# A decoder trunk step with the FFN's gate and up projections done as pairs of tiles by seven quarter products

## The chip, the cores and the metric

The kernel runs on one core of a Trainium2 chip. Its time is the device time of one execution in microseconds (us). PE is the matmul engine, DVE the vector engine (VectorE), ACT the scalar engine (ScalarE), POOL GpSimd, SP the engine whose queue issues the DMAs. L173 is line 173 of the kernel before.

## The reference, cut to what matters

Two layers of a decoder trunk are computed for 512 prompt tokens and 8 x 8 sample tokens, 576 columns in all, in float32. Layer 0 has a Conformer and window attention mixer, layer 1 a Mamba-2 mixer. Each layer ends with the same feed-forward block (FFN), with D_MODEL = 1024 and D_FF = 2816 (22 tiles of 128):

```python
def conv_ffn(h, hist, w_gate, w_up, conv_w, conv_b, w_down):
    gate = h @ w_gate
    padded = jnp.concatenate([hist, gate], axis=1)
    gc = causal_dwconv(padded, conv_w, conv_b)
    y = (jax.nn.silu(gc) * (h @ w_up)) @ w_down
    return y, padded[:, -(FFN_CONV_WIDTH - 1):]
```

h is the RMS-normalised input, and the convolution along the tokens has three taps.

## The kernel before

Channels lie on the 128 partitions and the 576 tokens along the free axis, cut into two halves of 288 (HALF). The residual stream x is 8 tiles of 128x576. Every large product is made of three matmuls: operand and weight are each split into a high part in float32r (a copy on ACT) and a low part (the difference, on DVE), and `mm3` (L167) adds high x high (L173), high x low (L174) and low x high (L175) over the input blocks.

A weight tile of 128x1024 comes by one DMA on SP's queue into one of three raw tiles (`wr`, L152). `weights` (L157) makes its high part on ACT (L163, tile `wh`) and its low part on DVE (L164, tile `wl`); `wh` and `wl` have three buffers each.

`units` (L270) computes output tiles: for each, eight input blocks, two halves, three matmuls, thus 48 matmuls of 128x288, into PSUM banks that take turns (`pm`, ring "mm" of four). In the FFN (L312) the input pairs `self.h` are x times the norm's gain, and the norm's factor per token, `rs`, is applied when a tile leaves PSUM. `gate_evac` (L322) multiplies by rs into `gbuf` (L329, L333, L334), runs the three taps on DVE (L339, then L341 twice), the SiLU on ACT (L344, L345) and multiplies by rs once more for the up branch (L347). `up_evac` (L351) multiplies the up tile into it (L354) and splits y into a pair (L193, L194). Gates run three tiles ahead of ups. After 8, 15 and 22 tiles (PARTS, L24) `out_proj` (L290) adds the part's share of the down projection to x: 16 tiles, each added on DVE at L288. In layer 0 the last part also computes the next norm.

The program is written in an order; the framework then orders each engine's instructions once, at build time, by that order and by when it takes operands to be ready, and sets the semaphores. The order on an engine can differ from the written one, unless a matmul is held by `keep_in_program_order`. Small tiles come from a list of numbered slots (`S`, `free`), where the slot that was freed first is taken first.

## Time and profile before

| | |
|---|---|
| median of 3 runs | 1552.0 us (1550.88 to 1556.76) |
| profiled execution, span | 1551.3 us; the page gives no other time of it |
| PE busy | 1520.5 us, 11635 matmuls |
| DVE busy | 1018.5 us, 1805 instructions |
| ACT busy | 649.3 us, 1232 instructions |
| first FFN | about 220 to 632 us of the span |
| second FFN | 1127 to 1548 us of the span |

Matmuls overlap in PE's pipeline, so a matmul's listed duration is longer than the distance to the next one, and PE's busy time doesn't tell whether it is at its peak; the distance between starts does. The same holds in part for DVE.

### The profile page before, as it was taken

How to read it: one execution, taken by the hardware profiler on the slowest of the kernel's cores; microseconds unless marked ns; L12 is line 12 of the kernel's file. 1: busy time of each engine (PE TensorE's matmuls, PEld its weight loads, DVE VectorE, ACT ScalarE, POOL GpSimd, SP SyncE). 2: the span in 40 equal slices, each digit the busy share in tenths (PEclk: the TensorE clock that was granted, in tenths of full speed). 3: DMA queues.
4: the chain of work that ended last, by engine and by line, in shares of the span. 5: the costliest groups of instructions: out<-in, count | busy, mean ns of one | idle time of the engine just before them, and what ended most of it. 6: DMA issues, size and time to landing. Idle time of an engine off the chain costs nothing.

```text
span 1551.3 us, 28549 instructions
## 1 busy us (share of the span) xinstructions
PE 1520.5 (98%) x11635; PEld 1449.8 (93%) x11635; DVE 1018.5 (66%) x1805; ACT 649.3 (42%) x1232; POOL 154.7 (10%) x365
## 2 busy tenths in 40 slices
PE   8999999999999999999999999999999999999999
PEld 7977799999999999898988988998999999999999
DVE  7969887553555464678896786777976644663552
ACT  6356553221222222486855654646632222321220
POOL 0036001000000000011211112102010000000000
PEclk9999999999999999999999999999999999999999
DMA  8515223222222222136245245245222222223222
GB/s 239 136 42 131 85 70 98 86 86 85 83 77 78 92 82 85 55 104 202 71 148 180 83 115 185 72 125 173 87 84 85 91 83 82 82 73 92 82 87 75
DMA packets 69938, 157.80 MB, mean 102 GB/s; under 512 B 19871, under 2 KB 24607, under 8 KB 69807
## 3 DMA queue, kind: packets, MB, share of 16 engines
q1 hardware_dynamic: 69806, 155.97, 33.2%
q8 instruction: 92, 1.51, 0.4%
q14 instruction: 40, 0.32, 0.1%
HBM read 140.73 MB, written 15.21 MB: 101 GB/s over the span
## 4 chain that ended last, share of the span: by engine, by line
PE 88%; DVE 5%; ACT 4%; DMA 2%; issue 1%; SPq 0%; ACTq 0%; DVEq 0%
PE mm L173 27%; PE mm L175 27%; PE mm L174 26%; DMA acb<-acd 2%; PE yp L1148 1%; DVE wl L164 1%; ACT acb L1116 1%; PE mm L594 1%; ACT wh L163 1%; PE pst L1081 1%; PE pt L1063 1%; ACT sm L661 1%; PE py L1133 1%; PE pst L1200 1%; DMA out_ssm_s<-h 1%
## 5 line engine op out<-in xcount | busy, mean ns | idle before, releaser
L173 PE MATMUL mm<-hh,wh 128*128 128x288 f32 x2272 | 677.8, 299 | 6.8 <-ACT wh L163 5.5
L174 PE MATMUL mm<-hl,wh 128*128 128x288 f32 x2272 | 673.9, 297 | 0.7 <-DVE hl L389 0.4
L175 PE MATMUL mm<-hh,wl 128*128 128x288 f32 x2272 | 673.3, 297 | 0.5 <-DVE wl L164 0.4
L163 ACT ACTIVATE wh<-wr 128x1024 fp32r<-128x1024 f32 (+2 forms) x215 | 223.3, 1039 | 544.6 <-PE mm L174 275.1
L173 PEld LDWEIGHTS mm<-hh,wh 128*128 128x128 f32 x2272 | 428.3, 189 | 16.0 <-ACT wh L163 6.0
L174 PEld LDWEIGHTS mm<-hl,wh 128*128 128x128 f32 x2272 | 429.0, 189 | 4.8 <-issue 1.8
L175 PEld LDWEIGHTS mm<-hh,wl 128*128 128x128 f32 x2272 | 428.7, 189 | 3.2 <-issue 1.4
L164 DVE TENSOR_TENSOR wl<-wr,wh 128x1024 fp32r<-128x1024 f32 (+2 forms) x215 | 258.6, 1204 | 73.0 <-ACT wh L163 71.4
L173 PE MATMUL mm<-yh,wh 128*128 128x288 f32 x960 | 285.9, 298 | 1.5 <-DVE x L288 1.4
L175 PE MATMUL mm<-yh,wl 128*128 128x288 f32 x960 | 284.2, 297 | 1.3 <-DVE wl L164 1.3
L174 PE MATMUL mm<-yl,wh 128*128 128x288 f32 x960 | 285.3, 297 | 0.0
L173 PEld LDWEIGHTS mm<-yh,wh 128*128 128x128 f32 x960 | 181.1, 189 | 5.7 <-DVE x L288 2.5
L175 PEld LDWEIGHTS mm<-yh,wl 128*128 128x128 f32 x960 | 181.1, 189 | 2.4 <-DVE wl L164 1.6
L174 PEld LDWEIGHTS mm<-yl,wh 128*128 128x128 f32 x960 | 181.2, 189 | 1.5 <-issue 1.0
L288 DVE TENSOR_TENSOR x<-x,mm 128x288 f32<-128x288 f32 x192 | 84.9, 449 | 143.0 <-PE mm L175 142.8
L333 DVE TENSOR_TENSOR gbuf<-mm,rs 128x224 f32<-128x224 f32 x44 | 17.2, 391 | 108.6 <-PE mm L175 108.6
L344 ACT ACTIVATE gsilu<-gconv,par 128x512 f32<-128x512 f32 x44 | 31.8, 724 | 115.1 <-DVE gconv L341 115.1
L341 DVE SCALAR_TENSOR_TENSOR gconv<-gbuf,par,gconv 128x592 f32<-128x592 f32 x88 | 73.1, 831 | 1.5
L354 DVE TENSOR_TENSOR gsilu<-mm,gsilu 128x288 f32<-128x288 f32 x88 | 40.0, 454 | 50.5 <-PE mm L175 50.5
L880 DVE SCALAR_TENSOR_TENSOR cconv<-cbuf,par,cconv 128x600 f32<-128x600 f32 x72 | 59.6, 838 | 10.1 <-ACT cconv L878 9.5
L336 POOL COPY fpo<-gbuf 128x2 f32<-128x2 f32 x44 | 12.4, 281 | 476.0 <-DVE gbuf L333 476.0
L1116 ACT ACTIVATE acb<-acb,ac 128x128 f32<-128x128 f32 x128 | 41.4, 390 | 35.6 <-DMA acb<-acd 25.0
(322 smaller groups left out, 1593.6 us busy)
## 6 DMA issues: line engine op xcount, KB each, us to landing
wr<-in_w_gate SPq DMA_DIRECT2D x44, 512.0 KB, 3.5
wr<-in_w_up SPq DMA_DIRECT2D x44, 512.0 KB, 3.5
wr<-in_w_in_o SPq DMA_DIRECT2D x40, 512.0 KB, 3.6
wr<-in_w_down SPq DMA_DIRECT2D x32, 448.0 KB, 3.3
wr<-in_w_down SPq DMA_DIRECT2D x16, 512.0 KB, 3.5
h<-in_h SPq DMA_DIRECT2D x32, 256.0 KB, 3.1
acb<-acd SPq DMA_DIRECT2D x32, 256.0 KB, 4.2
out_ssm_s<-h SPq DMA_DIRECT2D x32, 256.0 KB, 2.6
```

What stands on the lines that cost most here:

```text
L163: nc.scalar.activation(hi[:, a:b], raw[:, a:b], AF.Copy)
L164: nc.vector.tensor_tensor(lo[:, a:b], raw[:, a:b], hi[:, a:b].bitcast(F32), op=SUB)
L173: nc.tensor.matmul(out, hi[:, ws], xh[:, sl], start=i == 0, stop=False)
L174: nc.tensor.matmul(out, hi[:, ws], xl[:, sl], start=False, stop=False)
L175: nc.tensor.matmul(out, lo[:, ws], xh[:, sl], start=False, stop=i == n - 1)
L288: nc.vector.tensor_tensor(self.x[m][:, sl], self.x[m][:, sl], p[:, :HB], op=ADD)
L333: nc.vector.tensor_tensor(g[:, 290:514], p[:, 0:224], rs[:, HB:NP], op=MUL)
L341: nc.vector.scalar_tensor_tensor(cv[:, :592], g[:, k:592 + k], w(k), cv[:, :592], op0=MUL, op1=ADD)
L344: nc.scalar.activation(sl[:, :NP], cv[:, :NP], AF.Silu, bias=b)
L354: nc.vector.tensor_tensor(sl[:, HALF[half]], p[:, :HB], sl[:, HALF[half]], op=MUL)
L880: nc.vector.scalar_tensor_tensor(cv[:, :600], g[:, k:600 + k], w(k), cv[:, :600], op0=MUL, op1=ADD)
L1116: nc.scalar.activation(acb[:, cs], acb[:, cs], AF.Relu, bias=ac[:, o:o + 1], scale=-1.0)
```

## The change

Six tiles of each FFN are computed as before: gates 0 to 3 and ups 0 and 1. All other gate and up tiles are computed in pairs f, f+1. The pair's weights are seen as a 2x2 matrix of quarters A11, A12 (tile f, input blocks 0-3 and 4-7), A21, A22 (tile f+1), and the input as quarters B11, B21 (blocks 0-3 and 4-7, first half of the tokens), B12, B22 (second half). Strassen's scheme in Winograd's form needs seven products of quarters instead of eight. Each is 4 blocks x 3 matmuls of 128x288.

- `combine` makes, once per FFN, the seven quarters of the input from the normalised x (with rs): four as they are or as differences (B11, B21, B22, T1), then T2, T3, T4, each split into high and low. Its three stages stand between the lead tiles.
- Per pair, `load` makes four sums of weight quarters (S1 to S4) on DVE; seven quarters are split (the upper tile as one tile of 1024, A22 by itself, S1 and S2 in one tile, S4 and S3 in one).
- Two products accumulate on each of the banks z, y and x, where x takes three (P6, P7, P4); between them DVE or ACT reads what is there (`r`, `e`, `a`). The gate and up evacuations become sums; the first convolution tap goes from DVE to ACT; rs drops out for the tiles from 2 on.
- The products of two successive pairs are interleaved: P1 new, P3 and P7 old, P2 and P5 new, P4 old, P6 new. The down projection is in parts of 4, 4, 4, 4 and 6 tiles. The first four are cut into 16 single tiles each, and a tile is put after P1, P3, P7 and P5 once a part of y is complete; the first matmul of each product and of each such tile keeps its place in the order. The last part goes through `out_proj` as before.
- A down weight tile now holds two output tiles of four blocks and comes by two DMAs. The "mm" ring has six banks in the FFN.

```diff
-PARTS = ((0, 8), (8, 15), (15, 22))
+LEAD_G, LEAD_U = 4, 2
+PARTS = ((0, 4), (4, 8), (8, 12), (12, 16), (16, 22))
...
+class Strassen:
+    def __init__(self, b, job, n):
+        self.b, self.nc, self.job = b, b.nc, job
+        s = b.sr
+        self.r, self.e, self.a = s[0][:, HALF[n % 2]], s[1][:, HALF[0]], s[1][:, HALF[1]]
+    def load(self):
+        b, nc = self.b, self.nc
+        low, up = b.weights_load(self.job.src[1], 1024), b.weights_load(self.job.src[0], 1024)
+        a11, a12, a21, a22 = up[:, 0:512], up[:, 512:1024], low[:, 0:512], low[:, 512:1024]
+        self.up = up
+        s1, s2, s3, s4 = self.s = [b.S(f"st{i}", 512) for i in range(4)]
+        nc.vector.tensor_tensor(s1, a21, a22, op=ADD)
+        self.d = b.S("dh", 512, F32R), b.S("dl", 512, F32R)
+        self.split(a22, *self.d)
+        nc.vector.tensor_tensor(s3, a11, a21, op=SUB)
+        nc.vector.tensor_tensor(s2, s1, a11, op=SUB)
+        nc.vector.tensor_tensor(s4, a12, s2, op=SUB)
+    def split(self, src, hi, lo):
+        nc = self.nc
+        nc.scalar.activation(hi, src, AF.Copy)
+        nc.vector.tensor_tensor(lo, src, hi.bitcast(F32), op=SUB)
+    def tiles(self):
+        return [self.b.wp.tile([P, 1024], F32R, tag=t, bufs=3, name=t) for t in ("wh", "wl")]
+    def alpha(self):
+        self.w1 = self.tiles()
+        self.split(self.up, *self.w1)
+    def two(self, first, second):
+        w = self.tiles()
+        for i, t in enumerate((first, second)):
+            self.split(t, *(x[:, i * 512:i * 512 + 512] for x in w))
+        self.b.free(first, second)
+        return w
+    def beta(self):
+        self.w2 = self.two(self.s[0], self.s[1])
+    def gamma(self):
+        self.w3 = self.two(self.s[3], self.s[2])
+    def product(self, bank, w, col, q, first):
+        nc = self.nc
+        out = bank[:, :HB]
+        hi, lo = w
+        skip = not first
+        for k, t in enumerate(self.b.hq[q]):
+            ws = slice(col + k * P, col + k * P + P)
+            xh, xl = t[:, 0:HB], t[:, HB:T]
+            m = nc.tensor.matmul(out, hi[:, ws], xh, start=first and k == 0, stop=False, skip_group_check=skip)
+            if k == 0:
+                self.b.tc.keep_in_program_order(m)
+            nc.tensor.matmul(out, hi[:, ws], xl, start=False, stop=False, skip_group_check=skip)
+            nc.tensor.matmul(out, lo[:, ws], xh, start=False, stop=k == 3, skip_group_check=skip)
+    def p1(self):
+        self.z = self.b.hold("z")
+        self.product(self.z, self.w1, 0, "B11", True)
+        self.nc.scalar.activation(self.r, self.z[:, :HB], AF.Copy)
+    def p2(self):
+        self.product(self.z, self.w1, 512, "B21", False)
+        self.job.c11(self.z[:, :HB])
+        self.b.give(self.z)
+    def p5(self):
+        self.y = self.b.hold("y")
+        self.product(self.y, self.w2, 0, "T1", True)
+        self.nc.vector.tensor_tensor(self.e, self.r, self.y[:, :HB], op=ADD)
+    def p6(self):
+        self.x = self.b.hold("x")
+        self.product(self.x, self.w2, 512, "T2", True)
+        self.nc.vector.tensor_tensor(self.a, self.r, self.x[:, :HB], op=ADD)
+    def p3(self):
+        self.product(self.y, self.w3, 0, "B22", False)
+        self.job.c12(self.a, self.y[:, :HB])
+        self.b.give(self.y)
+    def p7(self):
+        self.product(self.x, self.w3, 512, "T3", False)
+        self.job.c22(self.e, self.x[:, :HB])
+    def p4(self):
+        self.product(self.x, self.d, 0, "T4", False)
+        self.job.c21(self.r, self.x[:, :HB])
+        self.b.give(self.x)
+        self.b.free(list(self.d))
...
     NSLOT = 48
-    EXTRA = 11
+    EXTRA = 17
 
...
+    def hold(self, name):
+        b = self.rings["mm"].pop(0)
+        t = self.pp.tile([P, 512], F32, tag=f"b{b}", bufs=1, name=name)
+        self.held[id(t)] = (b, t)
+        return t
+    def give(self, t):
+        self.rings["mm"].append(self.held.pop(id(t))[0])
...
     def weights_load(self, src, n):
         raw = self.wp.tile([P, 1024], F32, tag="wr", bufs=3, name="wr")
-        self.nc.sync.dma_start(raw[:, :n], src)
+        srcs = src if isinstance(src, list) else [src]
+        for i, s in enumerate(srcs):
+            self.nc.sync.dma_start(raw[:, i * n // len(srcs):(i + 1) * n // len(srcs)], s)
         return raw
...
-    def mm3(self, out, w, blocks, xs, sl, m=P):
+    def mm3(self, out, w, blocks, xs, sl, m=P, pin=False):
...
-            nc.tensor.matmul(out, hi[:, ws], xh[:, sl], start=i == 0, stop=False)
+            first = nc.tensor.matmul(out, hi[:, ws], xh[:, sl], start=i == 0, stop=False)
+            if pin and i == 0:
+                self.tc.keep_in_program_order(first)
...
+        nc = self.nc
+        q = self.hq[name] = [self.S("hq" + name, T, F32R) for _ in range(4)]
+        for t, src in zip(q, srcs):
+            nc.scalar.activation(t[:, 0:HB], src, AF.Copy)
+            nc.vector.tensor_tensor(t[:, HB:T], src, t[:, 0:HB].bitcast(F32), op=SUB)
+    def combine(self):
+        nc, (a, b) = self.nc, HALF
+        self.hq = {}
+        hf = [self.S("hf") for _ in range(8)]
+        u, v = hf[:4], hf[4:]
+        def scaled(k, sl):
+            nc.vector.scalar_tensor_tensor(hf[k][:, sl], self.x[k][:, sl], self.pv(self.gname, k), self.rs[:, sl], op0=MUL, op1=MUL)
+        def minus(out, x, y):
+            nc.vector.tensor_tensor(out, x, y, op=SUB)
+        for k in range(4):
+            scaled(k, a)
+        self.quarter("B11", [t[:, a] for t in u])
+        for k in range(4):
+            scaled(k, b)
+            minus(u[k][:, a], u[k][:, b], u[k][:, a])
+        self.quarter("T1", [t[:, a] for t in u])
+        yield
+        for k in range(4, 8):
+            scaled(k, a)
+        self.quarter("B21", [t[:, a] for t in v])
+        for k in range(4, 8):
+            scaled(k, b)
+        self.quarter("B22", [t[:, b] for t in v])
+        yield
+        for k in range(4):
+            minus(u[k][:, b], v[k][:, b], u[k][:, b])
+            minus(v[k][:, b], v[k][:, b], u[k][:, a])
+        self.quarter("T2", [t[:, b] for t in v])
+        self.quarter("T3", [t[:, b] for t in u])
+        for k in range(4):
+            minus(v[k][:, a], v[k][:, a], v[k][:, b])
+        self.quarter("T4", [t[:, a] for t in v])
+        self.free(hf)
+        yield
...
+        self.rings = {"mm": [0, 1, 2, 3, 4, 5], "aux": [6, 7]}
...
+        def gate_open(f):
+            g = gbuf[f] = self.S("gbuf", 594)
+            nc.gpsimd.memset(g[:, 0:2], 0.0)
+            nc.gpsimd.tensor_copy(samples(g)[:, :, 0:2], hist[:, f * 16:f * 16 + 16].rearrange("p (b c) -> p b c", c=2))
+            return g
+        def gate_done(f):
...
+            cv = self.S("gconv", 594)
+            w = lambda k: self.pv(f"fw{l}", f * 3 + k)
+            nc.scalar.activation(cv[:, :592], g[:, 0:592], AF.Copy, scale=w(0))
+            for k in (1, 2):
+                nc.vector.scalar_tensor_tensor(cv[:, :592], g[:, k:592 + k], w(k), cv[:, :592], op0=MUL, op1=ADD)
+            sl = sl_of[f] = self.S("gsilu")
+            b = self.pv(f"fb{l}", f)
...
+            if f < LEAD_U:
+                nc.vector.tensor_tensor(sl, sl, rs, op=MUL)
+            self.free(g, cv)
+
+        def up_done(f):
+            y_of[f] = self.pair("y")
+            self.split(sl_of[f], y_of[f])
+            self.free(sl_of.pop(f))
+
+        def lead_gate(f):
             def go(half, p):
                 if half == 0:
...
+                    nc.vector.tensor_tensor(gate_open(f)[:, 2:290], p[:, :HB], rs[:, :HB], op=MUL)
...
-                nc.vector.tensor_scalar(cv[:, :592], g[:, 0:592], w(0), None, op0=MUL)
...
-                nc.vector.tensor_tensor(sl, sl, rs, op=MUL)
...
+                nc.vector.tensor_tensor(samples(g)[:, :, 2:10], bt(p[:, 224:288]), bt(rs[:, NP:]), op=MUL)
+                gate_done(f)
...
-        for a, b in PARTS:
-            for f in range(a, b):
-                self.units([U(f)] + ([G(f + lead)] if f + lead < NF else []), 1)
-            last = b == NF
...
+        class Gate:
+            def __init__(me, f):
+                me.f, me.src = f, [d["w_gate"][l, f], d["w_gate"][l, f + 1]]
+            def c11(me, z):
+                nc.scalar.activation(gate_open(me.f)[:, 2:290], z, AF.Copy)
+            def second(me, f, u, v):
+                g = gbuf[f]
+                nc.vector.tensor_tensor(g[:, 290:514], u[:, 0:224], v[:, 0:224], op=ADD)
+                nc.vector.tensor_tensor(samples(g)[:, :, 2:10], bt(u[:, 224:HB]), bt(v[:, 224:HB]), op=ADD)
+            def c12(me, u, v):
+                me.second(me.f, u, v)
+                gate_done(me.f)
+            def c22(me, u, v):
+                gate_open(me.f + 1)
+                me.second(me.f + 1, u, v)
+            def c21(me, u, v):
+                nc.vector.tensor_tensor(gbuf[me.f + 1][:, 2:290], u, v, op=ADD)
+                gate_done(me.f + 1)
+        class Up:
+            def __init__(me, f):
+                me.f, me.src = f, [d["w_up"][l, f], d["w_up"][l, f + 1]]
+            def c11(me, z):
+                s = sl_of[me.f][:, :HB]
+                nc.vector.tensor_tensor(s, z, s, op=MUL)
+            def part(me, f, half, u, v):
+                nc.vector.tensor_tensor(u, u, v, op=ADD)
+                s = sl_of[f][:, HALF[half]]
+                nc.vector.tensor_tensor(s, s, u, op=MUL)
+            def c12(me, u, v):
+                me.part(me.f, 1, u, v)
+                up_done(me.f)
+            def c22(me, u, v):
+                me.part(me.f + 1, 1, u, v)
+            def c21(me, u, v):
+                me.part(me.f + 1, 0, u, v)
+                up_done(me.f + 1)
+        self.units([lead_gate(f) for f in range(3)], 3)
+        sums = self.combine()
+        next(sums)
+        self.units([lead_gate(3)], 1)
+        next(sums)
+        self.units([lead_up(0)], 1)
+        next(sums)
+        self.units([lead_up(1)], 1)
+        self.free(self.rs, self.h)
+        def down(p):
+            a, b = PARTS[p]
+            ys = [y_of[f] for f in range(a, b)]
+            for m in range(8):
+                if m % 2 == 0:
+                    w = self.weights([d["w_down"][l, m + i][:, a * P:b * P] for i in (0, 1)], 1024)
+                for half in (0, 1):
+                    t = self.pm()
+                    self.mm3(t[:, :HB], w, [(m % 2) * 4 + k for k in range(4)], ys, HALF[half], pin=True)
+                    self.add_x(m, half, t)
+                    if m == 7 and half == 1:
+                        self.free([y_of.pop(f) for f in range(a, b)])
+                    yield
+        todo = [Gate(LEAD_G), Up(LEAD_U)]
+        for f in range(LEAD_G + 2, NF, 2):
+            todo += [Gate(f), Up(f - 2)]
+        todo.append(Up(NF - 2))
+        self.sr = [self.S("st"), self.S("st")]
+        tiles = iter(())
+        ready = 0
+        def some(n):
+            for _ in range(n):
+                next(tiles, None)
+        prev = None
+        for n, job in enumerate(todo + [None]):
+            new = Strassen(self, job, n) if job else None
+            if prev:
+                prev.gamma()
+            if new:
+                new.load()
+                new.alpha()
+                new.p1()
+                some(1)
+            if prev:
+                prev.p3()
+                some(1)
+                prev.p7()
+                some(1)
+            if new:
+                new.p2()
+                new.beta()
+                new.p5()
+                some(1)
+            if prev:
+                prev.p4()
+            if new:
+                new.p6()
+            if ready < 4 and PARTS[ready][1] - 1 in y_of and n < len(todo):
+                some(16)
+                tiles = down(ready)
+                ready += 1
+            prev = new
+        some(16)
+        nc.sync.dma_start(d["ffn_s"][l], so)
+        nc.sync.dma_start(d["ffn_p"][l], po)
+        self.free(so, hist, self.sr, list(self.hq.values()))
+        if next_norm:
+            self.norm_begin(*next_norm)
+        a, b = PARTS[-1]
+        self.out_proj([d["w_down"][l, m][:, a * P:b * P] for m in range(8)], [y_of[f] for f in range(a, b)],
+                      b - a, next_norm is not None, next_norm is None)
+        self.free([y_of.pop(f) for f in range(a, b)])
...
-    nc = bacc.Bacc("TRN2", target_bir_lowering=False, num_devices=1)
+    nc = bacc.Bacc("TRN2", target_bir_lowering=False, num_devices=1, dynamic_dma_scratch_size=1024)
```

## The prediction, before the change was run

> **What bounds the kernel now.** I read the page's engine shares and the chain of waits first, then the two FFN stretches by windows, then the timeline of PE and VectorE (DVE) in the second FFN.

> ```profile
> span 1551.3 us, 28549 instructions
> PE 1520.5 (98%) x11635; PEld 1449.8 (93%) x11635; DVE 1018.5 (66%) x1805; ACT 649.3 (42%) x1232; POOL 154.7 (10%) x365
> PE 88%; DVE 5%; ACT 4%; DMA 2%; issue 1%; SPq 0%; ACTq 0%; DVEq 0%
> ```
> ```profile
> 1128.00:1548.00 420.00, 419.71 (x3173) 419.02 (x3171) 219.10 (x344) 104.66 (x139) 15.89 (x73) 1.00 0.27 84
> 220.00:632.00 412.00, 412.00 (x3110) 411.23 (x3109) 219.07 (x346) 109.98 (x150) 15.74 (x75) 1.00 0.27 83
> ```
> ```profile
> 1127.05 0.30 PE L173 MATMUL mm<-hh,wh 128*128 128x288 f32 x1
> ...
> 1547.41 0.29 PE L175 MATMUL mm<-yh,wl 128*128 128x288 f32 x1
> ```

> In the windows the columns after the length are PE, PEld, DVE, ACT and POOL busy, the granted clock, the DMA share and GB/s. In both FFNs PE never rests and the clock is 1.00; DVE is busy for 219 us of 420 (52%), ACT for 105 to 110. From its first gate matmul to its last down matmul an FFN takes 420.4 us. It has 44 gate and up tiles x 48 matmuls and 1056 down matmuls, 3168 in all, so one costs **0.1327 us**. So PE sets the end, and a matmul less is 0.1327 us less, as long as DVE keeps up.

> **What is removed.** Per pair of output tiles 96 matmuls of 128x288 become 84 (seven quarter products of 12). There are 9 gate and 10 up pairs per FFN, two FFNs: 38 x 12 x 0.1327 = **60.5 us**, the most that the change can bring. Down keeps its matmuls. That a second product accumulates on a bank already read has no row; its matmuls have the same shape, so I cost it at the same spacing. The least is no extra; the most is one evacuation of 0.45 us (L288's row below, 449 ns) per accumulated product if the bank's reader were late. In the new order two products or more lie between two on one bank, 1.59 us each (12 x 0.1327), so I take nothing.

> **What VectorE gets.** What one instruction takes of the engine is the step from its start to the next one's start in a busy stretch, which is shorter than the listed duration:

> ```profile
> 1113.43 0.45 DVE L229 TENSOR_TENSOR ssq<-ssq,sq 128x288 f32<-128x288 f32 x1
> 1113.80 0.80 DVE L288 TENSOR_TENSOR x<-x,mm 128x288 f32<-128x288 f32 x2
> 1114.53 1.21 DVE L164 TENSOR_TENSOR wl<-wr,wh 128x1024 fp32r<-128x1024 f32 x1
> 1115.66 0.50 DVE L249 SCALAR_TENSOR_TENSOR hl<-x,par,hh 128x288 fp32r<-128x288 f32 x1
> 1116.09 0.44 DVE L229 TENSOR_TENSOR ssq<-ssq,sq 128x288 f32<-128x288 f32 x1
> ...
> 1142.97 1.70 DVE L341 SCALAR_TENSOR_TENSOR gconv<-gbuf,par,gconv 128x592 f32<-128x592 f32 x2
> 1144.59 0.38 DVE L333 TENSOR_TENSOR gbuf<-mm,rs 128x224 f32<-128x224 f32 x1
> 1144.89 0.21 DVE L334 TENSOR_TENSOR gbuf<-mm,rs 128x64 f32<-128x64 f32 x1
> 1145.02 1.21 DVE L164 TENSOR_TENSOR wl<-wr,wh 128x1024 fp32r<-128x1024 f32 x1
> ...
> 1150.44 0.75 DVE L347 TENSOR_TENSOR gsilu<-gsilu,rs 128x576 f32<-128x576 f32 x1
> 1151.11 0.52 DVE L339 TENSOR_SCALAR gconv<-gbuf,par 128x592 f32<-128x592 f32 x1
> ```
> ```profile
> 717.49 0.68 DVE L1118 TENSOR_TENSOR acb<-acb,cbm 128x512 f32<-128x512 f32 x1
> 718.10 0.68 DVE L1089 TENSOR_TENSOR hst<-hst,cd 128x512 f32<-128x512 f32 x1
> 718.70 0.55 DVE L1137 TENSOR_TENSOR ea<-ea,py 128x384 f32<-128x384 f32 x1
> ```

> Steps: 288 wide 0.37, 288 with three operands 0.43, 512 wide 0.60, 1024 wide 1.13, a convolution tap 0.81, 224 wide 0.30, 64 wide 0.13, 576 wide 0.67. A gate pair then takes: four weight sums and five low parts of 512 (5.40), one low part of 1024 (1.13), two sums with r (0.74), evacuation 2 x 0.43 + 0.37 (1.23), four taps (3.24): **11.7 us**. An up pair: 6.53 + 0.74 + 0.37 + 3 x 0.74 + two y splits (1.34): **11.2 us**. PE needs 84 x 0.1327 = 11.15 for a pair. The first three pairs run without down tiles, since the first part of y is complete only then; the other 16 have four down tiles each, 48 matmuls more: PE 17.5, DVE about 11.5 + 4 x 0.37 + 1.13 = 14.1 (80%). So after the third pair DVE isn't the bound. What leaves DVE, the first tap (0.45, goes to ACT) and the product with rs (0.67), is not in these sums.

> ```profile
> L163 ACT ACTIVATE wh<-wr 128x1024 fp32r<-128x1024 f32 x181 | 191.5, 1059 | 431.1 <-issue 215.3 <-PE mm L174 211.3 <-DMA h<-in_h 1.8
> L344 ACT ACTIVATE gsilu<-gconv,par 128x512 f32<-128x512 f32 x44 | 31.8, 724 | 115.1 <-DVE gconv L341 115.1
> L193 ACT ACTIVATE yh<-gsilu 128x576 fp32r<-128x576 f32 x44 | 29.4, 669 | 0.0
> L288 DVE TENSOR_TENSOR x<-x,mm 128x288 f32<-128x288 f32 x192 | 84.9, 449 | 143.0 <-PE mm L175 142.8
> ```
> ```profile
> wr<-in_w_gate SPq DMA_DIRECT2D x44, 512.0 KB, 3.5
> ```

> In these groups the last number before the second bar is the mean ns of one. ACT has, per pair with its down tiles, the worth of 4.5 copies of 1024 (4.8 us) and for a gate pair two first taps and two activations (some 4), so at most 10 of 17.5 us. DMA bytes are the same, with 16 more issues per FFN on SP's queue; a raw tile lands 3.5 us after issue, and its buffer is free most of a pair ahead, so this I cost at nothing; without that lead it would be up to 3.5 us per pair.

> **Term 1, the front.** Six lead tiles keep PE for 288 x 0.1327 = 38.2 us, from 1127.05 to 1165.3. DVE is held by the norm until 1134:

> ```profile
> 1133.51 0.46 DVE L214 TENSOR_TENSOR dg<-rv,rsc 128x288 fp32r<-128x288 f32 x1
> 1134.20 0.46 DVE L329 TENSOR_TENSOR gbuf<-mm,rs 128x288 f32<-128x288 f32 x1 [0.23 <-PE mm L175]
> ```

> What then waits for it: four gate tiles (4.22, or 3.55 for the two that leave out the product with rs, three weight splits and one evacuation done by then: 11.8), two up tiles (5.1), and combine: 16 scalings x 0.43 + 16 differences x 0.37 + 28 low parts x 0.37 = 23.2. That is 40.1 us, and 34.7 for three pairs: 1134.0 + 74.8 = 1208.8. PE is through the same work at 1165.3 + 33.5 = 1198.8. The gap is 10.0 us. Taps and splits of the last pairs, some 5 us, can come later; served oldest first, PE instead waits already before the first product, some 13 us. Bounds 5 and 15 us, I take the gap itself, **10 us** per FFN.

> **Term 2, the weight buffers.** The rings wh and wl have three tiles, and a pair with down tiles uses four (w1, down, w2, w3). The down weights of pair n+1 take the tile of w2 of pair n, which the last product before the new pair frees; they are wanted one product later. The same hand-over stands in the trace, where a gate tile takes over a weight tile:

> ```profile
> 1140.36 0.29 PE L175 MATMUL mm<-hh,wl 128*128 128x288 f32 x1
> 1140.49 0.29 PE L173 MATMUL mm<-hh,wh 128*128 128x288 f32 x1
> ```
> ```profile
> 1140.61 1.06 ACT L163 ACTIVATE wh<-wr 128x1024 fp32r<-128x1024 f32 x1 [5.47 <-PE mm L174]
> ...
> 1141.39 0.53 DVE L339 TENSOR_SCALAR gconv<-gbuf,par 128x592 f32<-128x592 f32 x1
> 1141.84 1.22 DVE L164 TENSOR_TENSOR wl<-wr,wh 128x1024 fp32r<-128x1024 f32 x1
> ```

> From 1140.49, the first matmul after the old tile's last, the high part is ready at 1141.67 and the low part, had DVE been free, 1.22 later: 2.4 to 2.5 us. The down tile's third matmul, which needs it, is due after 14 x 0.1327 = 1.86. So each pair waits at least 0.6 us; behind older DVE work it is more. The trace shows the split put ahead of the convolution taps (L164 at 1141.84, L341 only at 1142.97), so I take 0.7 and not 0.6 plus a convolution. 16 x 0.7 = **11 us** per FFN; bounds 0 (the buffer comes free otherwise) and 2.3 per pair (0.7 + two taps of 0.81). Queued behind the stalled matmul on PE are three further products of that pair; behind the late low part on DVE the sums of the next.

> **Term 3, the tail.** The last part has six y tiles and the last comes from the last product: evacuation 0.74, copy 0.67, low part 0.67, about 2.1, against 15 matmuls (2.0) of its first down tile that don't need it: up to **1 us**.

> **Sum.** -60.5 + 2 x (10 + 11 + 1) = **-16.5 us**. The page gives the profiled execution's span, 1551.3, and no other time of it; the median of the runs is 1552.0, 0.7 above. 1552.0 - 16.5 = **1535**.

> **Rivals.** (a) **VectorE serves the oldest first.** The low part of the down weights, and that of the next w1, then queue behind taps and sums already ready: in a gate's pair behind two taps (0.7 + 1.62 = 2.3), in an up's behind a split and its product (0.7 + 0.67 + 0.37 = 1.7), mean 2.0. With a front of 13: 16 x 2.0 + 13 + 1 = 46 per FFN, 60.5 less than 92: **1584**. It decides from (30.25 - 11) / 16 = 1.2 us per pair. For it speaks DVE at 80% with an order fixed beforehand; against it the order at 1141.84. Longer waits in the front would slow the clock too, as here, where PE was busy for 0.54 us of two and then got half its clock:

> ```profile
> 648.00:650.00 2.00, 0.54 (x3) 0.22 (x2) 0.99 (x3) 0.69 (x3) 0.00 (x0) 1.00 0.32 127
> 650.00:652.00 2.00, 1.79 (x10) 1.79 (x11) 1.81 (x5) 1.42 (x4) 0.00 (x0) 0.75 0.00 0
> 652.00:654.00 2.00, 2.00 (x10) 2.00 (x10) 2.00 (x6) 0.49 (x2) 0.00 (x0) 0.50 0.00 0
> ```

> With the clock at 0.50, 10 matmuls stand in two microseconds where 15 fit, 0.7 us lost, and about as much in the two before: 1.4 per such stop. Three per FFN would add 8 us to the total. Waits of 0.7 us are far from it. (b) **Durations, not steps.** If each DVE instruction held the engine for its listed time, a gate pair is 13.25 (nine of 512 at 0.68, 1.23, two 0.455, evacuation 1.67, four 0.83), an up pair 12.9, lead and combine 51.2, so the front's gap is 22 and the total 60.5 against 2 x (22 + 11 + 1) = 68: **1560**. [...] The steps above, 0.37 for a listed 0.45, speak against it. (c) **Only a short front stays.** The order fills every gap, the front is 6, the buffers hide their hand-over: -60.5 + 2 x 7 = **1505**. Against it stands the ring's count of three.

> **Chances.** Forecast (1517 to 1546 by its bounds) 0.49, (a) 0.25, (b) 0.09, (c) 0.17. The likeliest time is 1535. Both signs hold much of the chance, so the range goes from just above (c) to short of (a)'s middle, **1506 to 1578**; below and above lie 0.07 and 0.13. A measurement tells 0.5%, 7.8 us, from no change. Above 1544 lie a little of the forecast, (a) and (b): faster 0.60, same 0.13, slower 0.27.

> **What would show it.** FFN: 2940 matmuls instead of 3168 at 0.133. The front: PE idle of some 10 us behind DVE between the third lead tile and the fourth pair. Steady: once per pair, PE waits about 0.7 us at the first down tile for the low part of the down weights; if those waits are 2 us, (a) holds. DVE near 80% in the pairs and steps of 0.60 at 512; a DVE over 95% there with steps of 0.68 is (b). I am wrong if PE's waits fall on the products' weights w1 or w2, on PSUM banks or on DMA instead.

## The result, and the profile after

The changed kernel takes **1559.9 us** (median of four, 1557.9 to 1564.8) against 1551.7 (1550.9 to 1556.8) for the kernel before on the same chip: a ratio of 1.005, 95% interval 1.0029 to 1.0071. It is slower by half a per cent. The prediction said faster, 1535, and its range, up to 1578, holds the time. The profiled execution is the longest of the four, 1564.8, so its span is some 5 us above what the median would have. Its page:

```profile
span 1562.8 us, 28458 instructions
PE 1482.2 (95%) x11179; PEld 1400.8 (90%) x11179; DVE 1246.2 (80%) x2327; ACT 799.0 (51%) x1546; POOL 180.0 (12%) x365
PEclk9999998999999999999999999999989999999999
L287 PE MATMUL mm<-hh,wl 128*128 128x288 f32 x1056 | 317.3, 302 | 22.3 <-DVE wl L274 22.3
L287 PE MATMUL mm<-yh,wl 128*128 128x288 f32 x960 | 288.1, 300 | 24.3 <-DVE wl L274 24.3
```

There are 456 matmuls fewer (11635 before), as the change says, but PE no longer works for 98% of the span. The last two rows say where it stands still: before the matmul that needs a weight tile's low part (`wl`, a subtraction on DVE at L274, L164 before), for 22.3 us where the input is the normalised x (`hh`; 20.9 of it at lead tiles of the two FFNs) and for 24.3 us at down tiles (`yh`). The clock row has two slices below 9, one in each FFN.

The second FFN by the starts of its matmuls, from the timeline of PE (first matmul, first product, last matmul):

```profile
1132.69 0.29 PE L283 MATMUL mm<-hh,wh 128*128 128x288 f32 x1
...
1186.47 0.30 PE L106 MATMUL z<-hqB,wh 128*128 128x288 f32 x1
...
1558.92 0.29 PE L287 MATMUL mm<-yh,wl 128*128 128x288 f32 x1
```

It takes 426.2 us, 2940 matmuls at the 0.1327 of before are 390.1, so 36.1 us are lost (pairs are counted from 1; a pair runs from its first product to the next pair's):

| part of the second FFN | takes | matmuls x 0.1327 | lost |
|---|---|---|---|
| six lead tiles (1132.69 to 1186.47) | 53.8 | 38.2 | 15.6 |
| up to the second pair | 8.5 | 6.4 | 2.1 |
| pairs 2 and 3, without down tiles | 22.3 | 22.3 | 0.0 |
| 16 pairs with down tiles | | | 18.2 (0.6 to 1.9 each) |
| the last part of down | | | 0.2 |

The first FFN loses 36.7 in the same places. So 60.5 us are saved and 73 lost, where before about 2 were.

**The front.** Windows of 10 us (after the length: PE, PEld, DVE, ACT, POOL busy, granted clock, DMA share, GB/s), then DVE and PE in the timeline:

```profile
1140.00:1150.00 10.00, 10.00 (x78) 10.00 (x77) 9.98 (x26) 5.23 (x11) 0.86 (x2) 1.00 0.01 2
1150.00:1160.00 10.00, 10.00 (x76) 9.82 (x75) 9.92 (x22) 8.03 (x15) 3.19 (x5) 1.00 0.15 52
1160.00:1170.00 10.00, 3.37 (x15) 3.31 (x15) 10.00 (x24) 6.40 (x17) 1.30 (x2) 0.63 0.18 53
1170.00:1180.00 10.00, 6.54 (x38) 6.31 (x38) 9.25 (x21) 4.14 (x9) 0.30 (x2) 0.84 0.02 2
```
```profile
1154.02 1.04 ACT L273 ACTIVATE wh<-wr 128x1024 fp32r<-128x1024 f32 x1
...
1163.08 0.94 DVE L370 SCALAR_TENSOR_TENSOR hf<-x,par,rs 128x288 f32<-128x288 f32 x2
1163.94 1.55 DVE L359 TENSOR_TENSOR hqB<-hf,hqB 128x288 fp32r<-128x288 f32 x4
1165.42 1.22 DVE L274 TENSOR_TENSOR wl<-wr,wh 128x1024 fp32r<-128x1024 f32 x1
...
1159.76 0.29 PE L286 MATMUL mm<-hl,wh 128*128 128x288 f32 x1
1166.69 0.61 PE L287 MATMUL mm<-hh,wl 128*128 128x288 f32 x1 [6.63 <-DVE wl L274]
...
1175.24 0.29 PE L287 MATMUL mm<-hh,wl 128*128 128x288 f32 x1
1178.99 0.40 PE L287 MATMUL mm<-hh,wl 128*128 128x288 f32 x1 [3.46 <-DVE wl L274]
```

DVE is busy for 29.9 of the 30 us from 1140 to 1170. The weights of up tile 0 have their high part at 1155.1 (ACT), but the low part starts only at 1165.42, behind convolution taps and the second stage of combine (L370 scalings, L359 low parts). PE stops for 6.8 us, and again for 3.6 at up tile 1. After each stop it runs slowly: the windows show a clock of 0.63 and 0.84. At half clock matmuls stand 0.24 apart (below, under hardware); 6.1 us and 3.4 us of work at that spacing lose 0.107 / 0.24 of their time, about 4.2 us. Stops and slow clock together are 14.6 of the 15.6.

In the first pair PE stops once more, between P1 and P2. Waits of PE from 1132 to 1195, and ACT in the timeline:

```profile
PE mm L287 <- DVE wl L274: 10.1, 2, 6.6
PE z L106 <- ACT st L115: 1.9, 1, 1.9
```
```profile
1187.51 0.63 ACT L75 ACTIVATE dh<-wr 128x512 fp32r<-128x512 f32 x1 [3.00 <-DMA wr<-in_w_gate]
1188.05 1.13 ACT L75 ACTIVATE wh<-st 128x512 fp32r<-128x512 f32 x2
1189.09 0.67 ACT L305 ACTIVATE yh<-gsilu 128x576 fp32r<-128x576 f32 x1
1189.66 0.39 ACT L115 ACTIVATE st<-z 128x288 f32<-128x288 f32 x1
```

P2 accumulates on z, which ACT must have read first (L115). P1's twelve matmuls start at 1186.47 and are through by 1188.2, but ACT reads only at 1189.66, after three weight copies and a y copy. In later pairs P3 and P7 of the old pair lie between P1 and P2; in the first there is no old pair.

**The down waits.** The short one of the pattern (pair 8), and the long one (pair 10), in the timeline:

```profile
1292.21 0.29 PE L106 MATMUL z<-hqB,wh 128*128 128x288 f32 x1
1292.28 1.06 ACT L273 ACTIVATE wh<-wr 128x1024 fp32r<-128x1024 f32 x1 [2.11 <-PE x L109]
1293.37 1.22 DVE L274 TENSOR_TENSOR wl<-wr,wh 128x1024 fp32r<-128x1024 f32 x1 [0.51 <-ACT wh L273]
1294.65 0.40 PE L287 MATMUL mm<-yh,wl 128*128 128x288 f32 x1 [0.42 <-DVE wl L274]
...
1328.82 0.29 PE L106 MATMUL z<-hqB,wh 128*128 128x288 f32 x1
1328.97 0.69 ACT L305 ACTIVATE yh<-gsilu 128x576 fp32r<-128x576 f32 x1 [2.21 <-DVE gsilu L569]
1329.56 1.04 ACT L273 ACTIVATE wh<-wr 128x1024 fp32r<-128x1024 f32 x1
1329.69 0.76 DVE L306 TENSOR_TENSOR yl<-gsilu,yh 128x576 fp32r<-128x576 f32 x1 [0.21 <-ACT yh L305]
1330.48 0.69 DVE L66 TENSOR_TENSOR st<-wr 128x512 f32<-128x512 f32 x1
1331.09 1.22 DVE L274 TENSOR_TENSOR wl<-wr,wh 128x1024 fp32r<-128x1024 f32 x1
1332.36 0.40 PE L287 MATMUL mm<-yh,wl 128*128 128x288 f32 x1 [1.17 <-DVE wl L274]
```

In pair 8 ACT starts the high part as the last product of the old pair ends, DVE follows at once, and the third matmul of the down tile is still 0.6 us late (1294.65 against 1292.21 + 14 x 0.1327 = 1294.07). In pair 10 a y split goes first on ACT, its low part and a weight sum go first on DVE, and the pair loses 1.8. From pair 4 on the pairs lose about 0.7, 1.0, 1.8 and 1.0 us in turn.

### The profile page after: what moved, and what is told of

Its sections match the earlier page's. It is cut to its first block, busy times and chain, and to the rows that moved or that the text cites. A ratio compares the mean times of both kernels' runs of the same rounds, so it can differ in the third digit from the quotient of the medians.

```text
span 1562.8 us, 28458 instructions
## 1 busy us (share of the span) xinstructions
PE 1482.2 (95%) x11179; PEld 1400.8 (90%) x11179; DVE 1246.2 (80%) x2327; ACT 799.0 (51%) x1546; POOL 180.0 (12%) x365
## 5 line engine op out<-in xcount | busy, mean ns | idle before, releaser
L287 PE MATMUL mm<-hh,wl 128*128 128x288 f32 x1056 | 317.3, 302 | 22.3 <-DVE wl L274 22.3
L283 PE MATMUL mm<-hh,wh 128*128 128x288 f32 x1056 | 321.9, 306 | 7.2 <-ACT wh L273 5.4
L286 PE MATMUL mm<-hl,wh 128*128 128x288 f32 x1056 | 318.8, 303 | 1.2 <-DVE hl L667 0.9
L287 PE MATMUL mm<-yh,wl 128*128 128x288 f32 x960 | 288.1, 300 | 24.3 <-DVE wl L274 24.3
L287 PEld LDWEIGHTS mm<-hh,wl 128*128 128x128 f32 x1056 | 203.7, 193 | 25.5 <-DVE wl L274 23.4
L283 PEld LDWEIGHTS mm<-hh,wh 128*128 128x128 f32 x1056 | 203.3, 193 | 15.2 <-ACT wh L273 5.4
L273 ACT ACTIVATE wh<-wr 128x1024 fp32r<-128x1024 f32 (+2 forms) x139 | 142.2, 1024 | 141.8 <-PE mm L286 98.7
L287 PEld LDWEIGHTS mm<-yh,wl 128*128 128x128 f32 x960 | 181.2, 189 | 32.8 <-DVE wl L274 31.8
L286 PEld LDWEIGHTS mm<-hl,wh 128*128 128x128 f32 x1056 | 203.4, 193 | 5.7 <-issue 1.7
L274 DVE TENSOR_TENSOR wl<-wr,wh 128x1024 fp32r<-128x1024 f32 (+2 forms) x139 | 167.6, 1208 | 47.6 <-ACT wh L273 46.5
L76 DVE TENSOR_TENSOR wl<-st,wh 128x512 fp32r<-128x512 f32 x152 | 101.2, 687 | 18.2 <-ACT wh L75 12.8
L106 PE MATMUL z<-hqB,wh 128*128 128x288 f32 x304 | 89.8, 295 | 4.2 <-ACT st L115 4.2
L106 PE MATMUL x<-hqT,wh 128*128 128x288 f32 x304 | 89.8, 295 | 0.0
L109 PE MATMUL x<-hqT,wh 128*128 128x288 f32 x304 | 89.7, 295 | 0.0
L109 PE MATMUL z<-hqB,wh 128*128 128x288 f32 x304 | 89.6, 295 | 0.0
## 6 DMA issues: line engine op xcount, KB each, us to landing
wr<-in_w_gate SPq DMA_DIRECT2D x44, 512.0 KB, 3.5
wr<-in_w_up SPq DMA_DIRECT2D x44, 512.0 KB, 3.5
wr<-in_w_in_o SPq DMA_DIRECT2D x40, 512.0 KB, 3.5
wr<-in_w_out_o SPq DMA_DIRECT2D x16, 512.0 KB, 3.6
```

Of the source, the lines that this page charges most:

```text
L76: nc.vector.tensor_tensor(lo, src, hi.bitcast(F32), op=SUB)
L106: m = nc.tensor.matmul(out, hi[:, ws], xh, start=first and k == 0, stop=False, skip_group_check=skip)
L109: nc.tensor.matmul(out, hi[:, ws], xl, start=False, stop=False, skip_group_check=skip)
L273: nc.scalar.activation(hi[:, a:b], raw[:, a:b], AF.Copy)
L274: nc.vector.tensor_tensor(lo[:, a:b], raw[:, a:b], hi[:, a:b].bitcast(F32), op=SUB)
L283: first = nc.tensor.matmul(out, hi[:, ws], xh[:, sl], start=i == 0, stop=False)
```

## The experiments

Each is timed against the kernel before (B) on the same chip. Experiments 1 to 4 start from the changed kernel (A), 5 to 7 from experiment 4.

**1. The first down tile after P2 instead of after P1.** Same work, same buffers; the down weights are wanted later in the pair. The rivals are that the waits come from the hand-over of the weight buffer (H), or that DVE is too full in the pairs (V).

```diff
                 new.p1()
-                some(1)
...
                 new.p2()
+                some(1)
                 new.beta()
```

> The changed kernel with one edit: of the four down tiles of a pair the first stands after P2 instead of after P1, so two more products lie between the last use of the w2 tile and the down weights that take it over. Theory H (hand-over of the weight ring): the wait at the down tile, 0.6 to 1.8 us in each of 32 pairs in the changed kernel, 36 us in all, goes; 1559.9 - 35 = 1525 (1518 to 1532), front unchanged at about 17.7 us per FFN. Rival V (VectorE, 80% busy in a fixed order, is late with whatever it makes): the waits move to P1, P5 or the next down tile, at most a third goes: 1548 or more.

Measured: 1527.2 us (1525.4 to 1530.8), ratio to B 0.9853 (0.9826 to 0.988). Four pairs in windows, of A and then of the experiment, columns as above:

```profile
1292.21:1366.57 74.36, 71.27 (x531) 70.10 (x529) 59.46 (x105) 31.47 (x50) 3.71 (x16) 1.00 0.27 86
```
```profile
1265.77:1335.95 70.18, 70.18 (x530) 70.01 (x529) 58.46 (x105) 31.34 (x50) 5.20 (x16) 1.00 0.29 91
```

Four pairs are 528 matmuls, 70.1 us; A takes 74.36, this one 70.18, with about as much DVE work in them (59.5 and 58.5 us). All but a few tenths of the 18 us per FFN are gone with DVE as full as before: H holds, V falls. The front still loses 16.7.

**2. The weights of gate 3, up 0 and up 1 ahead of the combine stage before them.** This moves their splits forward in the queues of ACT and DVE. The rivals are that the front's loss is a matter of order (O), or of the sum of DVE's work before the first products (W).

```diff
-        next(sums)
-        self.units([lead_gate(3)], 1)
-        next(sums)
-        self.units([lead_up(0)], 1)
-        next(sums)
-        self.units([lead_up(1)], 1)
+        for unit in (lead_gate(3), lead_up(0), lead_up(1)):
+            ready = [self.weights(unit[0], 1024)]
+            next(sums)
+            self.units([unit], 1, ready)
```

> The changed kernel with one edit: the weights of gate 3, up 0 and up 1 are split ahead of the stage of combine that stood before them. Theory O (oldest first on VectorE): the two waits of 6.8 and 3.6 us at the up tiles' low parts fall under 1 us each, the clock stays up longer, some of the wait comes back before the first product; the front falls from 17.7 to 10 to 12 us per FFN: 1547 (1541 to 1552). Rival W (the sum of VectorE's work sets the front whatever its order): the front stays within 3 us of 17.7: 1554 to 1562.

Measured: 1556.2 us (1554.6 to 1559.1), ratio 1.0029 (1.0016 to 1.0042). Waits of PE in the front:

```profile
PE z L110 <- DVE wl L76: 7.8, 1, 7.8
PE mm L287 <- DVE wl L274: 3.1, 1, 3.1
```

The 10 us at the up tiles become 3.1 there and 7.8 at the first product, whose own low part (L76) now stands behind combine. The lead tiles lose 5.5 and the first pair 11.4, 16.9 in all, as much as in A less 0.8. O falls: moving work within DVE's queue moves the wait.

**3. Both edits.**

> Both edits, the down tile after P2 and the lead weights ahead of combine. If H and O hold and do not overlap: 1559.9 - 35 - 12 = 1513 (1504 to 1522), faster than the kernel before by 2 to 3%. Under V and W: 1545 or more.

Measured: 1525.9 us (1522.5 to 1527.8), ratio 0.9835 (0.981 to 0.9859). The waits of PE in the front are those of experiment 2, 3.1 and 7.9 us. Neither time that was expected came, 1513 or 1545 and more, since H holds and O does not. The intervals of this run and of experiment 1 overlap, so no gain over it is shown: the edit that only moves a wait adds nothing to the one that removes the other.

**4. The split S1 and S2 in small slots of their own, not in a ring tile.** The order stays A's; a pair with down tiles now needs three tiles of the rings, which have three.

```diff
     def beta(self):
-        self.w2 = self.two(self.s[0], self.s[1])
+        b = self.b
+        self.w2 = []
+        for s in self.s[0:2]:
+            w = b.S("w2h", 512, F32R), b.S("w2l", 512, F32R)
+            self.split(s, *w)
+            b.free(s)
+            self.w2.append(w)
...
-        self.product(self.y, self.w2, 0, "T1", True)
+        self.product(self.y, self.w2[0], 0, "T1", True)
+        self.b.free(*self.w2[0])
...
-        self.product(self.x, self.w2, 512, "T2", True)
+        self.product(self.x, self.w2[1], 0, "T2", True)
+        self.b.free(*self.w2[1])
```

> The changed kernel with the order of the products and down tiles untouched, but the split S1 and S2 go to four small slots instead of a tile of the weight ring, so that the ring of three has three takers. Theory H: the down weights no longer wait for P6, the 36 us go as in the kernel with the later down tile, within 5 us of it: 1525 (1520 to 1532). Rival: the wait comes from VectorE's order or from the place of the down tile after P1: 1550 or more.

Measured: 1521.9 us (1520.0 to 1524.0), ratio 0.9812 (0.9789 to 0.9835). Four pairs in windows, and the waits of PE in the front:

```profile
1262.08:1332.24 70.16, 70.16 (x531) 70.16 (x529) 58.32 (x105) 31.67 (x50) 4.25 (x16) 1.00 0.27 91
```
```profile
PE mm L295 <- DVE wl L282: 10.5, 2, 6.6
PE z L112 <- ACT st L121: 0.8, 1, 0.8
```

The down tile stays where A has it, after P1, and PE does not wait: it was the buffer. This confirms H by another way, and the gain over A, 38 us, is what A lost in its 32 pairs (2 x 18.2 = 36.4), and a little. The front is as in experiment 1, 16.7 in the second FFN. (Lines are 8 further on here and below: L295 is A's L287, L282 its L274.)

**5. Combine without its 16 differences**, on top of experiment 4. It leaves out the subtractions of the input quarters, so that the products are of other quarters and the output is not the reference's; 16 x 0.37 = 5.9 us of DVE's work per FFN are gone, nothing else. W expects the front to shrink by that and more; its rival F expects it to stay.

```diff
         def minus(out, x, y):
-            nc.vector.tensor_tensor(out, x, y, op=SUB)
+            return
```

> The kernel with the split S1 and S2 in slots, and in combine the 16 differences of 0.37 us are left out (the T quarters are then made of plain halves, so the products are others; their count and every other instruction stay). Theory W (the sum of VectorE's work ahead of the first pairs sets the front): the front, 16.6 us per FFN before, falls by the 5.9 us left out and up to 3 more for less time at half clock: 1521.9 - 12 to 18 = 1504 to 1510. Rival F (a fixed chain sets it, ACT's copies, the norm's end or a DMA): less than 3 us per FFN, 1516 or more.

Measured: 1507.6 us (1504.8 to 1508.0), ratio 0.9715 (0.9695 to 0.9735). The waits of PE in the front:

```profile
PE mm L295 <- DVE wl L282: 5.4, 1, 5.4
```

The front loses 9.6 instead of 16.7. It shrinks by 7.1 for 5.9 us of work: one stop of the two is gone, and the clock is low for less long: a mean of 0.94 from 1102 to 1157, some 6.6 us at half, where A's front has 13.6 (below, under hardware). W holds, F falls.

**6. Ten lead tiles instead of six, the four new ones behind the last stage of combine**, on top of experiment 4. Per FFN two pairs less are done by quarter products (24 matmuls, 3.2 us).

```diff
-LEAD_G, LEAD_U = 4, 2
+LEAD_G, LEAD_U = 6, 4
...
         self.units([lead_up(1)], 1)
+        for f in (2, 3):
+            self.units([lead_gate(f + 2)], 1)
+            self.units([lead_up(f)], 1)
```

> The kernel with the split S1 and S2 in slots, with ten lead tiles instead of six, the four more behind the last stage of combine. PE gets 24 matmuls more per FFN (two pairs fewer, 3.2 us), VectorE about 11 us less, but all of it behind the waits at ups 0 and 1. Theory W with the oldest served first: those waits stay, so the front keeps some 13 to 16 us and the added matmuls come on top: 1522 to 1530. If only the balance over the whole front counted: 1505.

Measured: 1524.5 us (1523.4 to 1525.9), ratio 0.9829 (0.9807 to 0.9852). Waits of PE in the front:

```profile
PE mm L295 <- DVE wl L282: 8.0, 2, 7.3
PE z L112 <- ACT st L121: 3.4, 1, 3.4
```

The front loses 18.4 in the second FFN, 15.4 in the first. More PE work, put behind the place where PE waits, doesn't help it there.

**7. The same ten lead tiles, with the stages of combine spread between them**, each behind the weights of the next lead tile.

```diff
-        next(sums)
-        self.units([lead_gate(3)], 1)
-        next(sums)
-        self.units([lead_up(0)], 1)
-        next(sums)
-        self.units([lead_up(1)], 1)
+        for unit, stage in ((lead_gate(3), 1), (lead_up(0), 0), (lead_up(1), 1), (lead_gate(4), 0), (lead_up(2), 1),
+                            (lead_gate(5), 0), (lead_up(3), 0)):
+            ready = [self.weights(unit[0], 1024)]
+            if stage:
+                next(sums)
+            self.units([unit], 1, ready)
```

> The same ten lead tiles, but the stages of combine stand before gate 3, up 1 and up 2, each behind the split of the next lead tile's weights. Theory W: PE has 63.7 us of lead work against some 58 us of VectorE work from 7 us later, so the front's waits fall to 5 us or less and the clock stays up, for 3.2 us of matmuls more per FFN: 1521.9 - 2 x (16.6 - 5 - 3.2) = 1505 (1498 to 1512). Rival F: the waits stay, 1520 or more.

Measured: **1502.8 us** (1501.4 to 1508.2), ratio 0.9694 (0.967 to 0.9719). Its page, and its waits of PE in the front:

```profile
PE 1466.8 (98%) x11227; PEld 1395.4 (93%) x11227; DVE 1217.6 (81%) x2287; ACT 791.3 (53%) x1524; POOL 177.2 (12%) x365
```
```profile
PE mm L295 <- DVE wl L282: 2.1, 1, 2.1
PE z L112 <- ACT st L121: 0.7, 1, 0.7
```

PE is back at 98% and the front loses about 5 us. An added lead tile keeps PE for 48 x 0.1327 = 6.4 us and DVE, by the prediction's steps, for 2.5 (up) or 3.55 (gate); four give DVE some 13 us to catch up, and now they stand where it needs them. Two things differ from experiment 6, the spread of the stages and the weights put ahead of them; they were not run apart, but in experiments 2 and 3 the weights ahead brought nothing by themselves. This version beats both kernels, by 3.1% the one before and by 3.7% the changed one (1502.8 / 1559.9).

## Why the prediction was wrong

The mechanisms were the ones predicted; two terms of the sum were too small, and since both count twice, the sign turned. With either term measured and the other as predicted the sum is -1 to -2 us, no change; it took both.

- **The saving, 60.5 us: right.** Matmuls of a listed 0.29 to 0.30 us stand 0.1327 apart in all products where nothing is waited for (70.16 us for 528 in experiment 4), also on a bank that is accumulated on a second time.
- **Steps, not durations: right.** Two sums of 512 in the front with one low part of 512 between them, in the timeline of A:

```profile
1178.86 0.68 DVE L66 TENSOR_TENSOR st<-wr 128x512 f32<-128x512 f32 x1
...
1180.07 0.68 DVE L69 TENSOR_TENSOR st<-wr 128x512 f32<-128x512 f32 x1
```

  Each step is 0.60 (1.21 / 2) at a listed 0.68, which is against rival (b). That its time, 1560, is the measured one is coincidence: it has 22 us for the front and 11 for the pairs, where 17.7 and 18.2 were measured. (Its 22 also doesn't follow from the 51.2 beside it, which gives 25.8; 22 comes out with three weight splits and an evacuation taken off, as in term 1.) The low part between the two sums starts at 1179.46, 0.08 us before the listed end of the first.

  DVE is busy for 59.46 of 74.36 us in the pairs, the 80% of the forecast, but in part by luck: a pair holds 14.9 us of DVE work where 14.1 was added up, and the waits lengthen the pairs. In experiment 4, without these waits, DVE is at 83% (58.32 of 70.16).
- **Term 1, the front: 17.7 us where I took 10, and above its bound of 15.** The step that failed is the choice of the gap at the end of the third pair. I had the other case beside it: served oldest first, PE waits before the first product, "some 13 us". That is what DVE's queue does. The waits alone (10.4 at the up tiles, 2.1 at P2, and some 1 us beside) are 13.5 of the 17.7; the half clock behind the stops adds the other 4.2. The prediction named that slow clock under rival (a), at 1.4 us per stop, and left it out of the term. The 2.1 at P2 was ruled out under the saving by "two products or more lie between two on one bank", which is false for the first pair.
- **Term 2, the weight buffers: 1.14 us a pair where I took 0.7**, 18.2 per FFN instead of 11. The hand-over is as described and the pair without older work loses 0.63, the predicted minimum of 0.6. The step that failed is the reading of one row as the order of every pair: there the split was put ahead of the taps (1141.84), but in three pairs of four something older goes first on ACT or DVE, a y split, a weight sum or a tap. That is rival (a) on a small scale: half its price (2.0), just short of the 1.2 from which it would decide. Experiments 1 and 4 show the cause, from the side of the order and from that of the buffer.
- **Term 3, the tail: 0.3 instead of up to 1.** The last pair loses 1.18 where its like lose about 0.9.
- **The sum.** With the second FFN's measured terms for both: -60.5 + 2 x (17.7 + 18.2) = +11.3, and the spans differ by 1562.8 - 1551.3 = 11.5. The medians differ by 8.2, since the profiled execution of A is its longest.
- **Rival (c), 1505,** needed a front of 6 us and hidden buffers. Its time was reached only by experiment 7, which changes both places.

The odds were badly set too: slower had 0.27, most of it from (a)'s 2.0 us per pair. A loss of 15 us in the front and of 1.0 in the pairs, both inside the bounds given, already makes 2 x (15 + 16) = 62 against 60.5. The bounds were there; I did not add them up. The forecast's "1517 to 1546 by its bounds" is not what they give: with 15, 16 x 2.3 and 1 the sum is +45, 1597. And the measured front lies above its bound of 15.

What stays open is what each of the older instructions costs in the pairs of 1.0 and of 1.8; it was read from the timeline, not tested one by one.

## What to carry to other kernels

When matmuls are traded for VectorE work, count the trade where that work is due and not over the stage: here DVE was busy for only 80% in the steady pairs, and the loss came from the work due at the start, 40 us by the prediction's steps, and from a ring of buffers one tile short. A wait that is a sum of work is not cured by another order (experiment 2 moved it); it is cured by putting work of the other engine in front of it (7, but not 6). And add the upper bounds of all terms once, to see whether the sign survives them.

## What the runs showed of the hardware

**How long the clock stays low.** Short windows of A around its two stops in the front (1159.9 to 1166.7, 1175.4 to 1179.0):

```profile
1162.00:1164.00 2.00, 0.00 (x0) 0.00 (x0) 2.00 (x5) 1.21 (x3) 0.00 (x0) 0.65 0.01 4
...
1166.00:1168.00 2.00, 1.31 (x5) 1.31 (x6) 2.00 (x5) 0.97 (x3) 0.00 (x0) 0.50 0.24 25
...
1172.00:1174.00 2.00, 2.00 (x14) 2.00 (x13) 1.63 (x5) 0.35 (x1) 0.00 (x0) 0.79 0.00 0
1178.00:1180.00 2.00, 1.01 (x6) 1.01 (x7) 2.00 (x3) 0.37 (x1) 0.00 (x0) 0.92 0.10 12
...
1182.00:1184.00 2.00, 2.00 (x13) 2.00 (x13) 2.00 (x4) 0.13 (x2) 0.00 (x0) 0.73 0.69 231
```

```profile
1180.07 0.45 PE L287 MATMUL mm<-hh,wl 128*128 128x288 f32 x1
...
1182.47 0.45 PE L283 MATMUL mm<-hh,wh 128*128 128x288 f32 x1
```

Ten of them in 2.40 us, 1.8 and not 2 times the 0.1327. The clock fell 2.7 us after the stop of 6.8 us had begun, with PE still standing, and 4.3 us after the beginning of the stop of 3.6, when PE had been at work again for 0.7. In experiment 7 the stop of 2.3 us (about 1149.4 to 1151.7, a wait of 2.1 in its list above) was followed by a clock of 0.50 from 1152 to 1154; with 0.96 and 0.69 in the windows of 2 us on either side, the clock was at half from about 1151.8 to 1155.2, 3.4 us again. The stops before P2 in A were followed by none: after the one of 2.0 us in the second FFN (1188.1 to 1190.1) and the one of 2.5 us in the first (274.2 to 276.7) the windows have 1.00, up to 1214 and 300. So, by these stops, length alone doesn't settle it: 2.3 us drew half clock, 2.5 us did not. What else decides, these runs don't show. By these numbers, as an estimate, a stop of 2.3 or 3.6 us that draws one stretch at half clock costs, beside itself, up to 1.5 us (3.4 x 0.107 / 0.24), and the one of 6.8 us cost 2.7 (6.1 x 0.107 / 0.24).
